# Transposed dense products of a two-layer decoder: high weights against high and low tokens in one 512-column matmul

## The chip, the cores and the metric

The kernel runs on one core of a Trainium2 chip. The time is device microseconds of one launch, the median of three runs. The engines are TensorE (PE in the profile, with its weight loads as PEld), VectorE (DVE), ScalarE (ACT), GpSimd (POOL) and SyncE (SP), whose queue issues the big loads.

## The reference

Two layers over 256 tokens of width 2048, in 32-bit floating point: a retention layer (A) and a dilated attention layer (B), each with a branch that attends to 256 fixed memory tokens. Nearly all the arithmetic is in the dense products with the weights.

```python
D_MODEL = 2048; SEQ = 256; DEPTH = 2; MEM_LEN = 256      # BATCH = 1
...
def rmsnorm(x, g):
    xf = x.astype(jnp.float32)
    y = xf * lax.rsqrt(jnp.mean(xf * xf, axis=-1, keepdims=True) + EPS) * g.astype(jnp.float32)
    return y.astype(x.dtype)
...
def retention_layer(x, g, w_in, w_mem_kv, w_out, mem_n):
    h = rmsnorm(x, g)
    q, k, v, gate_r, mq, gate_m = split_cols(h @ w_in, [RET_QK_W, RET_QK_W, RET_V_W, RET_V_W, MEM_W, MEM_W])
    ...
    o = retention(q, k, v.reshape(B, S, RET_HEADS, RET_DV))
    o = o * lax.rsqrt(jnp.mean(o * o, axis=-1, keepdims=True) + EPS)
    o_ret = o.reshape(B, S, RET_V_W).astype(x.dtype) * jax.nn.silu(gate_r)
    o_mem = memory_branch(mq, gate_m, mem_n, w_mem_kv)
    return x + jnp.concatenate([o_ret, o_mem], axis=-1) @ w_out
...
def dilated_layer(x, g, w_in, w_mem_kv, w_out, mem_n, kv):
    h = rmsnorm(x, g)
    parts = split_cols(h @ w_in, [DIL_W] * n_g + [DIL_W, MEM_W, MEM_W])
    ...                  # three (window, dilation) groups, merged by their softmax denominators
    o_mem = memory_branch(mq, gate_m, mem_n, w_mem_kv)
    return x + jnp.concatenate([o_dil, o_mem], axis=-1) @ w_out
...
def reference(x, mem, norm_a, w_in_a, w_out_a, norm_b, w_in_b, w_out_b, w_mem_kv, mem_norm_g, kv_norm_g, w_kv, final_norm_g):
    mem_n = rmsnorm(mem, mem_norm_g)
    x = retention_layer(x, norm_a[0], w_in_a[0], w_mem_kv[0], w_out_a[0], mem_n)
    kv = shared_kv(x, kv_norm_g, w_kv)          # rmsnorm(x) @ w_kv, cut into keys and values
    x = dilated_layer(x, norm_b[0], w_in_b[0], w_mem_kv[1], w_out_b[0], mem_n, kv)
    return rmsnorm(x, final_norm_g)
```

## The kernel before

**Three matmuls for one product.** A 32-bit product is made of parts that TensorE takes at its fast rate (type fp32r): each operand is split into a high part and the low rest (`split`, L73: ScalarE copies to the high part, VectorE subtracts). A product is then high x high + high x low + low x high, three matmuls into one accumulator.

**Two kinds of dense product.** `dense` (L242) makes 512 output columns of the tokens times a weight matrix, over a contraction of 2048 (16 blocks of 128) or 3072 (the two out-projections). With `transposed=True`, called a *column product* here, the weights are the stationary operand and the 256 tokens stream: for each block of 128 x 512 weights there are four column groups (`ct`) with three matmuls of 256 columns each (`mm3`, L77 to L80). There are 44 such products. Otherwise, a *row product*, the tokens are stationary and 512 weight columns stream (`row_part`, L248 to L252).

**Weights.** `weights` (L216) loads raw tiles of 128 x 1024 (two blocks, 512 KB) through SyncE's queue into a ring of five (`wraw`), and splits each 512-wide block into a ring of four pairs (`wspl`: `wh`, `wl`). Where a norm's gain is folded into the weights (layer B: `w_b`, `w_kv`), ScalarE scales with a per-partition gain (L237) and VectorE subtracts with the same gain (L238); elsewhere a plain `split` is used. Splits are marked with a priority of 100, so the tile framework's scheduler moves them ahead of work that is written before them.

**Order of the work.** The products follow one another on TensorE. All the rest (attention, statistics, transposes) is written as generators in `pending`; after each weight block `step()` takes one piece from the first of them, so that attention's matmuls lie between those of the next products. Accumulators `acc` are four PSUM banks, a product takes two. At the end of a product its result leaves PSUM through `cols_plain`, `cols_plain2`, `cols_scaled`, `gate_cols` or `rotary` for column products.

**Sequence.** Memory keys of layer A (two column products, whose tokens arrive meanwhile: `SplitCols`, L168, splits them at L184 and L185), memory values, the same for layer B, then layer A's products with memory attention and `retention`, the out-projection with transposes of the result (`turn_cols`, L530) and the norm of layer B (`norm_y`, L630), then for each of four head groups three query and three key column products, three value row products and a gate, with `dilated` attention (L469) of one group lying beside the first column products of the next. The second out-projection and the final norm end the kernel.

## Time and profile before

| | |
|---|---|
| median of 3 runs | 1940.17 us (1940.11 to 1940.19) |
| profiled execution, first to last instruction (span) | 1937.8 us |
| what lies around the span, against the median | 2.4 us |
| TensorE busy | 1925.1 us (99%) |
| VectorE busy | 1181.4 us (61%) |
| ScalarE busy | 1054.4 us (54%) |
| mean granted TensorE clock | 0.998 |
| read from memory | 345.80 MB, 180 GB/s over the span |

The profiled execution's own time is its span; the few microseconds around it are the launch, and are taken from the median of the runs. Busy is the share in which an instruction of the engine was running. Matmuls are pipelined, so their durations overlap, and a busy TensorE isn't a TensorE at its peak: the pitch from one start to the next tells its pace.

### The profile page before, as it was taken

To read this page: it belongs to the slowest core of one execution; us is meant where nothing else is said; L and a number is where in the kernel's file an instruction comes from. 1 tells how busy PE (TensorE), PEld (TensorE's weight loads), DVE (VectorE), ACT (ScalarE), POOL (GpSimd) and SP (SyncE) were. 2 spreads that over 40 slices of the span, in tenths; PEclk is the share of its full clock that TensorE was granted. 3 is DMA by queue.
4 is the path that set the end of the run, shared out by engine and by line. 5 is a ranking of instruction groups with operands and counts; after the bars stand their busy time and mean duration, and the time that the engine had idled before them with its cause. 6 is when DMAs were issued, how large, how long until landed. Compare 5 with 4: busy or idle time off the path is not lost.

```text
span 1937.8 us, 33224 instructions
## 1 busy us (share of the span) xinstructions
PE 1925.1 (99%) x12952; PEld 1785.4 (92%) x12952; DVE 1181.4 (61%) x1871; ACT 1054.4 (54%) x1731; POOL 12.2 (1%) x24
## 2 busy tenths in 40 slices
PE   9999999999999999999999999999999999999998
PEld 9898999889888889999989999899998999989886
DVE  6666557667666566665556655566555665556754
ACT  6556445555555455555555555555555555556544
POOL 0000000000000000000000000000000000000000
PEclk9999999999999999999999999999999999999999
DMA  7565544554555555445554355553555535555454
GB/s 267 184 228 187 184 159 159 203 181 167 200 186 199 202 185 175 164 163 177 185 195 175 134 183 184 196 175 131 185 178 194 183 134 181 182 195 175 150 200 144
DMA packets 98909, 350.06 MB, mean 181 GB/s; under 512 B 11088, under 2 KB 11648, under 8 KB 98752
## 3 DMA queue, kind: packets, MB, share of 16 engines
q1 hardware_dynamic: 98288, 347.12, 51.5%
q8 instruction: 101, 1.65, 0.3%
q0 software_dynamic: 320, 0.81, 0.1%
q14 instruction: 56, 0.46, 0.1%
q10 hardware_dynamic: 144, 0.01, 0.0%
HBM read 345.80 MB, written 2.10 MB: 180 GB/s over the span
## 4 chain that ended last, share of the span: by engine, by line
PE 98%; issue 1%; DVE 0%; DMA 0%; ACT 0%; POOL 0%; SPq 0%; ACTq 0%; POOLq 0%; DVEq 0%
PE acc L79 17%; PE acc L80 17%; PE acc L78 17%; PE acc L252 13%; PE acc L250 13%; PE acc L251 13%; PE att L79 1%; PE att L80 1%; PE att L78 1%; PE att L499 1%; PE att L477 1%; PE att L513 1%; DMA big<-in_memt_dram 0%; PE att L536 0%; PE att L451 0%
## 5 line engine op out<-in xcount | busy, mean ns | idle before, releaser
L78 PE MATMUL acc<-big,wh 128*128 128x256 f32 x2816 | 803.1, 285 | 1.7 <-ACT big L184 1.7
L80 PE MATMUL acc<-big,wl 128*128 128x256 f32 x2816 | 797.9, 283 | 0.0
L79 PE MATMUL acc<-big,wh 128*128 128x256 f32 x2816 | 797.6, 283 | 0.3 <-DVE big L185 0.3
L238 DVE SCALAR_TENSOR_TENSOR wl<-raw,gain,wh 128x512 fp32r<-128x512 f32 x704 | 528.4, 751 | 410.2 <-ACT wh L237 407.9
L237 ACT ACTIVATE wh<-raw,gain 128x512 fp32r<-128x512 f32 x704 | 509.0, 723 | 443.7 <-PE acc L79 311.3
L75 DVE TENSOR_TENSOR wl<-raw,wh 128x512 fp32r<-128x512 f32 x564 | 388.4, 691 | 275.1 <-ACT wh L74 273.3
L78 PEld LDWEIGHTS acc<-big,wh 128*128 128x128 f32 x2816 | 540.9, 192 | 2.2 <-ACT big L184 1.9
L79 PEld LDWEIGHTS acc<-big,wh 128*128 128x128 f32 x2816 | 541.2, 192 | 0.8 <-DVE big L185 0.5
L80 PEld LDWEIGHTS acc<-big,wl 128*128 128x128 f32 x2816 | 540.9, 192 | 0.0
L74 ACT CAST wh<-raw 128x512 fp32r<-128x512 f32 x564 | 349.8, 621 | 346.8 <-DVE wl L75 175.9
L250 PE MATMUL acc<-wh,big 128*128 128x512 f32 x1128 | 441.5, 391 | 0.0
L251 PE MATMUL acc<-wl,big 128*128 128x512 f32 x1128 | 439.3, 389 | 0.0
L252 PE MATMUL acc<-wh,big 128*128 128x512 f32 x1128 | 439.2, 389 | 0.0
L252 PEld LDWEIGHTS acc<-wh,big 128*128 128x128 f32 x1128 | 211.7, 188 | 44.3
L251 PEld LDWEIGHTS acc<-wl,big 128*128 128x128 f32 x1128 | 211.9, 188 | 42.4
L250 PEld LDWEIGHTS acc<-wh,big 128*128 128x128 f32 x1128 | 211.9, 188 | 42.4
L485 ACT ACTIVATE p<-sm,mn 128x512 f32<-128x512 f32 x32 | 23.1, 721 | 21.3 <-DVE mn L481 21.2
L75 DVE TENSOR_TENSOR big<-big 128x512 fp32r<-128x512 f32 (+1 forms) x34 | 28.4, 846 | 9.8 <-ACT big L74 9.7
L78 PE MATMUL att<-big 128*128 128x256 f32 x112 | 31.9, 285 | 0.0
L80 PE MATMUL att<-big 128*128 128x256 f32 x112 | 31.7, 283 | 0.0
L79 PE MATMUL att<-big 128*128 128x256 f32 x112 | 31.7, 283 | 0.0
L74 ACT CAST big<-big 128x512 fp32r<-128x512 f32 (+1 forms) x34 | 24.9, 745 | 11.7 <-DVE big L391 6.5
(150 smaller groups left out, 815.2 us busy)
## 6 DMA issues: line engine op xcount, KB each, us to landing
raw<-in_w_kv_dram SPq DMA_DIRECT2D x192, 512.0 KB, 3.6
raw<-in_w_b_dram SPq DMA_DIRECT2D x160, 512.0 KB, 3.6
raw<-in_w_a_dram SPq DMA_DIRECT2D x128, 512.0 KB, 3.6
raw<-in_w_mem_dram SPq DMA_DIRECT2D x60, 512.0 KB, 4.3
raw<-in_w_oa_dram SPq DMA_DIRECT2D x48, 512.0 KB, 3.7
raw<-in_w_ob_dram SPq DMA_DIRECT2D x48, 512.0 KB, 4.3
raw<-in_w_mem_dram SPq DMA_DIRECT2D x8, 256.0 KB, 7.7
big<-in_xt_dram SPq DMA_DIRECT2D x4, 512.0 KB, 6.5
```

The costliest lines, as they stand in the source:

```text
L74: act.copy(hi, src)
L75: dve.tensor_tensor(lo, src, hi.bitcast(F32), ALU.subtract)
L78: pe.matmul(o, lhsT=ah, rhs=bh, start=first, stop=False, skip_group_check=True)
L79: pe.matmul(o, lhsT=ah, rhs=bl, start=False, stop=False, skip_group_check=True)
L80: pe.matmul(o, lhsT=al, rhs=bh, start=False, stop=last, skip_group_check=True)
L237: act.activation(wh, src, AF.Copy, scale=gs)
L238: dve.scalar_tensor_tensor(wl, src, gs, wh.bitcast(F32), ALU.mult, ALU.subtract)
L250: pe.matmul(ps[t], lhsT=hi[:, a, ts], rhs=wh, start=first, stop=False)
L251: pe.matmul(ps[t], lhsT=hi[:, a, ts], rhs=wl, start=False, stop=False)
L252: pe.matmul(ps[t], lhsT=lo[:, a, ts], rhs=wh, start=False, stop=last)
L477: pe.matmul(ps[:, P + i * P:2 * P + i * P], lhsT=q[i][:, hd, ts], rhs=k[i][:, hd, ts], start=False, stop=(i == 2), skip_group_check=True)
L485: act.activation(p, sm, AF.Exp, bias=mn, scale=-1.0, accum_out=ls)
```

## The change

**Tokens side by side.** The token operand of a column product is stored as [128, 2, 2, 256]: for a block of the contraction the high and the low tokens stand next to each other (`cols_pair`, `xh`, `xl`, `xhl`).

**Two matmuls instead of three.** `dense_cols` multiplies a 128 x 128 piece of the high weights with the high and low tokens in one matmul of 512 columns, into a whole PSUM bank, and the low weights with the high tokens in one of 256 columns into the bank's first half. The result is the sum of the bank's two halves: `fold` copies the low half out (ScalarE) and adds the high half (VectorE), and what followed before (scaling, gate, rotary, split) follows on the folded tile.

**Halves of a product.** A column product is now made in two halves of 256 output columns, each over the whole contraction and in two banks; `acc` holds two such tiles. A weight tile for it is 1024 columns wide, four contraction blocks of 256 columns, contiguous in memory. The split pairs are 1024 wide, in a ring of three instead of four of 512, the raw ring has six tiles instead of five. A tile without gains is split by one 1024-wide pair of instructions; one with gains needs four pairs of 256 in a column product and two of 512 in a row product. `step()` comes after each second block of 256 columns.

**Start.** The first four raw tiles hold the first half of the first product; all four parts of the memory tokens are loaded between them. The first result is folded without the norm's factor and scaled later (`scale_half`).

```diff
-LOAD = 2
-RAW = 5
+RAW = 6
...
-    wspl = ctx.enter_context(tc.tile_pool(name="wspl", bufs=4))
+    wspl = ctx.enter_context(tc.tile_pool(name="wspl", bufs=3))
...
-    acc = ctx.enter_context(tc.tile_pool(name="acc", bufs=4, space=bass.MemoryType.PSUM))
+    acc = ctx.enter_context(tc.tile_pool(name="acc", bufs=2, space=bass.MemoryType.PSUM))
...
+    def cols_pair():
+        return [big.tile([P, 2, 2, S], F32R, name="big") for _ in range(2)]
+
+    def xh(part, a):
+        return part[a // 2][:, a % 2, 0, :]
+
+    def xl(part, a):
+        return part[a // 2][:, a % 2, 1, :]
+
+    def xhl(part, a):
+        return part[a // 2][:, a % 2].rearrange("p h s -> p (h s)")
...
-    def weights(w, c, j, g, keep=False):
-        res = []
-        for i in range(4):
-            if i % LOAD == 0:
-                if loaded:
-                    raw = loaded.popleft()
-                else:
-                    raw = wraw.tile([P, LOAD, 512], F32, name="raw")
-                    sp.dma_start(out=raw, in_=w[c, j, :, i:i + LOAD, :])
...
+    def split_weights(src, g, k0, n, wh, wl):
+        with tc.high_priority(AHEAD):
+            if g is None:
+                split(wh, wl, src)
+                return
+            w = src.shape[-1] // n
+            for i in range(n):
+                cs = slice(i * w, (i + 1) * w)
+                gs = gain[:, g, k0 + i:k0 + i + 1]
+                act.activation(wh[:, cs], src[:, cs], AF.Copy, scale=gs)
+                dve.scalar_tensor_tensor(wl[:, cs], src[:, cs], gs, wh[:, cs].bitcast(F32), ALU.mult, ALU.subtract)
+
+    def weights(src, g, k0, n, keep=False):
+        fresh = not loaded
+        if fresh:
+            raw = wraw.tile([P, 1024], F32, name="raw")
+            sp.dma_start(out=raw, in_=src)
+        else:
+            raw = loaded.popleft()
...
+            wh = wspl.tile([P, 1024], F32R, name="wh")
+            wl = wspl.tile([P, 1024], F32R, name="wl")
+        w = 1024 // n
+        if fresh:
+            split_weights(raw, g, k0, n, wh, wl)
+        else:
+            for i in range(n):
+                cs = slice(i * w, (i + 1) * w)
+                split_weights(raw[:, cs], g, k0 + i, 1, wh[:, cs], wl[:, cs])
+        return [(wh[:, i * w:(i + 1) * w], wl[:, i * w:(i + 1) * w]) for i in range(n)]
+
+    def dense_cols(xs, w, c, evict, g=None):
+        for i in range(2):
+            ps = acc.tile([P, 2, 2, S], F32, name="acc")
+            for j in range(4):
+                part = xs[j]
+                for a, (wh, wl) in enumerate(weights(w[c, i, j], g, 4 * j, 4)):
+                    first, last = j == 0 and a == 0, j == 3 and a == 3
+                    for ct in range(2):
+                        cs = slice(ct * P, (ct + 1) * P)
+                        pe.matmul(ps[:, ct].rearrange("p h s -> p (h s)"), lhsT=wh[:, cs], rhs=xhl(part, a),
+                                  start=first, stop=False, skip_group_check=True)
+                        pe.matmul(ps[:, ct, 0, :], lhsT=wl[:, cs], rhs=xh(part, a),
+                                  start=False, stop=last, skip_group_check=True)
+                    if a % 2:
+                        step()
+            evict(i, ps)
...
-                if transposed:
-                    for ct in range(4):
-                        o = ps[ct // 2][:, (ct % 2) * S:(ct % 2 + 1) * S]
-                        cs = slice(ct * P, (ct + 1) * P)
-                        mm3(o, wh[:, cs], wl[:, cs], hi[:, a, :], lo[:, a, :], first and ct % 2 == 0, last and ct % 2 == 1)
...
+    def fold(out, ps):
+        act.copy(two(out), ps[:, :, 1, :])
+        dve.tensor_tensor(two(out), ps[:, :, 0, :], two(out), ALU.add)
...
-    def cols_scaled(ps, b):
+    def cols_scaled(b, *job):
         o = big_tile()
-        for i in range(2):
-            dve.tensor_tensor(two(half(o, i)), two(ps[i]), twice(b), ALU.mult)
+
+        def evict(i, ps):
+            fold(half(o, i), ps)
+            if b is not None:
+                scale_half(o, i, b)
+
+        dense_cols(*job[:3], evict, *job[3:])
         return o
...
+    for j in range(4):
+        loaded.append(wraw.tile([P, 1024], F32, name="raw"))
+        if j == 0:
+            for i in range(4):
+                sp.dma_start(out=ms.raw[0][:, i, :], in_=memt[:, 0, i, :])
+                sp.dma_start(out=loaded[0][:, i * S:(i + 1) * S], in_=w_mk[0, 0, 0, 0, :, i * S:(i + 1) * S])
+        else:
+            ms.load(j)
+            sp.dma_start(out=loaded[j], in_=w_mk[0, 0, 0, j])
...
-    ps = dense(ms, w_mem[0], 0, transposed=True)
+    mk0 = cols_scaled(None, ms, w_mk[0], 0)
```

What the scheduler makes of it, at three places. Numbers stand for the position in the engine's queue; the lines of the change are its own (L85 and L86 are the plain split, L137 a square of the statistics, L195 and L196 the split of the tokens, L236 and L237 the split of weights with a gain, L314 and L315 the fold).

ScalarE at the start of the kernel, before (L74 is the cast of a weight block, L126 a square of the memory tokens, L184 the split of the memory tokens):

```order
4 L74 CAST wh<-raw 128x512
5 L126 ACTIVATE sm<-big 128x512
6 L74 CAST wh<-raw 128x512
7 L184 ACTIVATE big<-big,gain 128x256 x2
8 L74 CAST wh<-raw 128x512
9 L184 ACTIVATE big<-big,gain 128x256
```
The same place in the change:

```order
4 L85 CAST wh<-raw 128x256
5 L137 ACTIVATE sm<-big 128x512
6 L85 CAST wh<-raw 128x256 x2
7 L137 ACTIVATE sm<-big 128x512
8 L85 CAST wh<-raw 128x256
9 L137 ACTIVATE sm<-big 128x512 x2
10 L85 CAST wh<-raw 128x256 x4
11 L195 ACTIVATE big<-big,gain 128x256 x5
12 L85 CAST wh<-raw 128x256 x4
```
The first token split stood behind two casts and one square; now it stands behind eight casts of 256 and four squares, and the last of the 16 behind a cast of 1024.

VectorE where layer B begins, before (L621 adds the out-projection to the residual, one for each half of the tokens, L632 begins the norm):

```order
370 L238 SCALAR_TENSOR_TENSOR wl<-raw,gain,wh 128x512 x2
371 L621 TENSOR_TENSOR big<-big,acc 128x512
372 L238 SCALAR_TENSOR_TENSOR wl<-raw,gain,wh 128x512
373 L621 TENSOR_TENSOR big<-big,acc 128x512
374 L238 SCALAR_TENSOR_TENSOR wl<-raw,gain,wh 128x512 x2
375 L632 TENSOR_REDUCE ss<-part 128x2
376 L147 TENSOR_SCALAR r_y<-ss 128x2
377 L154 TENSOR_SCALAR p<-ident,r_y 128x128
```
The same place in the change (L681 is the add, L692 begins the norm):

```order
337 L237 SCALAR_TENSOR_TENSOR wl<-raw,gain,wh 128x256 x8
338 L681 TENSOR_TENSOR big<-big,acc 128x512
339 L237 SCALAR_TENSOR_TENSOR wl<-raw,gain,wh 128x256 x4
340 L681 TENSOR_TENSOR big<-big,acc 128x512
341 L237 SCALAR_TENSOR_TENSOR wl<-raw,gain,wh 128x256 x4
342 L692 TENSOR_REDUCE ss<-part 128x2
343 L158 TENSOR_SCALAR r_y<-ss 128x2
344 L165 TENSOR_SCALAR p<-ident,r_y 128x128
345 L86 TENSOR_TENSOR big<-att,big 128x2x256 x2
```
Between the two adds stood one split of 512, now there are four of 256, a whole tile; four more follow ahead of the norm.

VectorE in dilated attention, before (L481 adds the mask and finds the minimum, L487 and L488 divide by the sum after ScalarE's exponent, L75 splits the transposed weights of attention):

```order
479 L481 ISA sm,mn<-att,mask_t,nsd_y 128x512
480 L481 ISA mn 128x1
481 L487 RECIPROCAL rl_11659<-ls_11657 128x1
482 L488 TENSOR_SCALAR p<-p,rl_11659 128x512
483 L238 SCALAR_TENSOR_TENSOR wl<-raw,gain,wh 128x512
484 L75 TENSOR_TENSOR pl<-att,ph 128x2x128
485 L238 SCALAR_TENSOR_TENSOR wl<-raw,gain,wh 128x512
```
The same in the change (L537, L543 and L544, L86):

```order
487 L537 ISA sm,mn<-att,mask_t,nsd_y 128x512
488 L537 ISA mn 128x1
489 L86 TENSOR_TENSOR pl<-att,ph 128x2x128
490 L543 RECIPROCAL rl_9454<-ls_9452 128x1
491 L544 TENSOR_SCALAR p<-p,rl_9454 128x512
492 L237 SCALAR_TENSOR_TENSOR wl<-raw,gain,wh 128x256 x4
```
Two splits of 512 in a unit have become four of 256 in one place; between the mask and the division, where VectorE waits for ScalarE, stands a split of attention at most.

## Rows read from the trace of the kernel before

**Rows 1.** The page: busy time by engine; the chain by engine.
```profile
PE 1925.1 (99%) x12952; PEld 1785.4 (92%) x12952; DVE 1181.4 (61%) x1871; ACT 1054.4 (54%) x1731; POOL 12.2 (1%) x24
...
PE 98%; issue 1%; DVE 0%; DMA 0%; ACT 0%; POOL 0%; SPq 0%; ACTq 0%; POOLq 0%; DVEq 0%
```

**Rows 2.** Groups by line: names, shapes, count | busy us, mean ns | idle before.
```profile
L78 PE MATMUL acc<-big,wh 128*128 128x256 f32 x2816 | 803.1, 285 | 1.7 <-ACT big L184 1.7
...
L79 PEld LDWEIGHTS acc<-big,wh 128*128 128x128 f32 x2816 | 541.2, 192 | 0.8 <-DVE big L185 0.5
```

**Rows 3.** Order in time (start us, us, what), TensorE, a column product.
```profile
900.02 0.28 PE L80 MATMUL acc<-big,wl 128*128 128x256 f32 x1
...
906.02 0.28 PE L79 MATMUL acc<-big,wh 128*128 128x256 f32 x1
```

**Rows 4.** Order in time, TensorE, a row product.
```profile
989.69 0.39 PE L250 MATMUL acc<-wh,big 128*128 128x512 f32 x1
...
999.89 0.39 PE L250 MATMUL acc<-wh,big 128*128 128x512 f32 x1
```

**Rows 5.** Windows: us; busy by PE PEld DVE ACT POOL; clock, DMA, GB/s.
```profile
880.00:900.00 20.00, 20.00 (x169) 20.00 (x168) 10.52 (x14) 11.02 (x17) 0.00 (x0) 1.00 0.51 182
...
980.00:1000.00 20.00, 20.00 (x90) 16.57 (x89) 12.25 (x17) 11.77 (x17) 0.00 (x0) 1.00 0.56 198
```

**Rows 6.** Splits in order of time, ScalarE then VectorE: 256 wide, 512 wide.
```profile
17.55 1.70 ACT L184 ACTIVATE big<-big,gain 128x256 fp32r<-128x256 f32 x4
...
18.36 1.67 DVE L185 SCALAR_TENSOR_TENSOR big<-big,gain 128x256 fp32r<-128x256 f32 x4
...
727.78 1.41 DVE L238 SCALAR_TENSOR_TENSOR wl<-raw,gain,wh 128x512 fp32r<-128x512 f32 x2
```

**Rows 7.** Groups by line: 1024-wide splits, evictions from PSUM.
```profile
L74 ACT CAST big<-big 128x1024 fp32r<-128x1024 f32 x10 | 10.4, 1045 | 3.0 <-DVE big L297 3.0
...
L75 DVE TENSOR_TENSOR big<-big 128x1024 fp32r<-128x1024 f32 x10 | 12.1, 1223 | 2.9 <-ACT big L74 2.9
...
L285 ACT COPY big<-acc 128x512 f32<-128x512 f32 x16 | 9.2, 576 | 0.9
...
L297 DVE TENSOR_TENSOR big<-acc,nb 128x512 f32<-128x512 f32 x32 | 20.5, 683 | 0.0
```

**Rows 8.** The start: token split; group to 11.94; matmul; window; DMA to 12.
```profile
6.64 0.91 ACT L184 ACTIVATE big<-big,gain 128x256 fp32r<-128x256 f32 x2
...
L78 PE MATMUL acc<-big,wh 128*128 128x256 f32 x8 | 2.8, 372 | 1.7 <-ACT big L184 1.7
...
11.95 0.28 PE L79 MATMUL acc<-big,wh 128*128 128x256 f32 x1
...
9.00:12.00 3.00, 3.00 (x16) 3.00 (x16) 1.09 (x2) 1.16 (x4) 0.00 (x0) 0.51 1.03 400
...
DMA packets 1889, 3.17 MB, mean 264 GB/s; under 512 B 373, under 2 KB 933, under 8 KB 1889
...
q0 software_dynamic: 320, 0.81, 22.5%
```

**Rows 9.** The turn to layer B in order of time: TensorE, VectorE.
```profile
719.59 0.64 PE L536 MATMUL att<-ident,big 128*128 128x128 f32 x4
...
722.31 0.29 DVE L154 TENSOR_SCALAR p<-ident,r_y 128x128 f32<-128x128 f32 x1 [0.80 <-POOL r_y L148]
```

**Rows 10.** Dilated attention: windows; VectorE in order of time.
```profile
1052.00:1064.00 12.00, 12.00 (x103) 11.82 (x102) 10.42 (x24) 8.29 (x18) 0.00 (x0) 1.00 0.43 154
...
1064.00:1076.00 12.00, 12.00 (x104) 12.00 (x104) 7.99 (x19) 6.95 (x15) 0.00 (x0) 1.00 0.25 89
...
1061.03 0.74 DVE L481 CUSTOM_DVE_ANT_0 sm<-att,mask_t,nsd_y 128x512 f32<-128x512 f32 x1
...
1062.66 0.17 DVE L487 RECIPROCAL rl<-ls 128x1 f32<-128x1 f32 x1 [0.88 <-ACT p L485]
...
1072.28 0.74 DVE L481 CUSTOM_DVE_ANT_0 sm<-att,mask_t,nsd_y 128x512 f32<-128x512 f32 x1
```

More of the change, by code (lines that the diff above doesn't have):

```diff
@@ L242, in dense @@
-    def dense(xs, w, c, g=None, transposed=False, order=(0, 1, 2, 3), both=None, after=None):
-        ps = [acc.tile([P, 512], F32, name="acc") for _ in range(2)]
+    def split_weights(src, g, k0, n, wh, wl):
[9 more added lines that the diff above has]
+                dve.scalar_tensor_tensor(wl[:, cs], src[:, cs], gs, wh[:, cs].bitcast(F32), ALU.mult, ALU.subtract)
@@ L244, in dense @@
+    def dense(xs, w, c, g=None, order=(0, 1, 2, 3), both=None, after=None):
+        pt = acc.tile([P, 2, 512], F32, name="acc")
+        ps = [pt[:, t, :] for t in range(2)]
         n = 4 * len(order)
@@ L256, in dense @@
                 drain()
-            hi, lo = xs[j]
-            keep = both is not None and k >= both
-            for a, (wh, wl) in enumerate(weights(w, c, j, g, keep)):
-                first, last = k == 0, k == n - 1
-                k += 1
-                if transposed:
-                    for ct in range(4):
-                        o = ps[ct // 2][:, (ct % 2) * S:(ct % 2 + 1) * S]
-                        cs = slice(ct * P, (ct + 1) * P)
-                        mm3(o, wh[:, cs], wl[:, cs], hi[:, a, :], lo[:, a, :], first and ct % 2 == 0, last and ct % 2 == 1)
-                else:
-                    row_part(0, hi, lo, a, wh, wl, first, last)
+            part = xs[j]
+            for u in range(2):
+                keep = both is not None and k >= both
+                for a, (wh, wl) in enumerate(weights(w[c, j, u], g, 4 * j + 2 * u, 2, keep), 2 * u):
+                    first, last = k == 0, k == n - 1
+                    k += 1
+                    row_part(0, part, a, wh, wl, first, last)
                     if keep:
-                        late.append((1, hi, lo, a, wh, wl, first, last))
+                        late.append((1, part, a, wh, wl, first, last))
                     else:
-                        row_part(1, hi, lo, a, wh, wl, first, last)
-                step()
-                if len(order) > 4 and k % 2 == 0:
+                        row_part(1, part, a, wh, wl, first, last)
                     step()
+                    if len(order) > 4 and k % 2 == 0:
+                        step()
         if after is not None:
@@ L324, in gate_rows, with gate_cols, evict @@
         return o
-    def gate_cols(ps, bh):
+    def gate_cols(bh, *job):
         o = big_tile()
-        for i in range(2):
+        def evict(i, ps):
             hv = half(o, i)
-            dve.tensor_tensor(two(hv), two(ps[i]), twice(bh), ALU.mult)
+            fold(hv, ps)
+            dve.tensor_tensor(two(hv), two(hv), twice(bh), ALU.mult)
             th = tmp.tile([P, 512], F32, name="sm")
@@ L333, in gate_cols, with rotary, evict @@
             dve.scalar_tensor_tensor(hv, th, 1.0, hv, ALU.add, ALU.mult)
+        dense_cols(*job[:3], evict, *job[3:])
         return o
-    def rotary(ps, cosr, sinr):
+    def rotary(cosr, sinr, *job):
         h, l = big_pair()
-        for i in range(2):
-            s_ = two(ps[i])
+        def evict(i, ps):
+            z = tmp.tile([P, 512], F32, name="p12")
+            fold(z, ps)
+            s_ = two(z)
             a = tmp.tile([P, 2, S], F32, name="p")
@@ L528, in dilated, with turn_cols @@
                 yield
-    def turn_cols(xr, h, l):
+    def turn_cols(xr, part):
         for i in range(2):
@@ L536, in turn_cols @@
                     pe.transpose(ps[:, ct * S + t * P:ct * S + (t + 1) * P], xr[:, t, cs], ident)
-            split(half(h, i), half(l, i), ps)
+            split(part[i][:, :, 0, :], part[i][:, :, 1, :], two(ps))
             yield
@@ L558, in stats_m @@
         yield
-        mk_a.append(split_big(cols_scaled(ps, n_m.b)))
+        for i in range(2):
+            scale_half(mk0, i, n_m.b)
+            yield
+        mk_a.append(split_big(mk0))
         yield
```

132 lines of the change are left out of this document (63 added, 69 removed).

## The prediction

> **What bounds the kernel now.** I read the page first: TensorE is busy 99% of the span and is 98% of the chain that ended last [rows 1]. Nothing else matters unless it makes TensorE wait, so the next view is what TensorE spends its time on. In the groups by line the matmuls of the dense products carry nearly everything: 2816 of each of L78, L79 and L80 with 256 moving columns, the column products, of which [rows 2] shows the first line; the row products (L250 to L252) stream 512. The mean durations (285 ns) overlap and must not be added: 8448 x 0.285 us is longer than the span. What counts is the pitch from one start to the next, which only the order in time shows. In a column product 50 matmuls start within 6.00 us, 0.1200 us each [rows 3]; in a row product 45 start within 10.20 us, 0.2267 us each [rows 4]. Twice the columns cost 0.1067 us more, so each matmul has a part of 0.1200 - 0.1067 = 0.0133 us that doesn't depend on its columns. The clock is granted in full in both stretches (1.00, the 2.4 GHz level) [rows 5].
>
> **Column products, the term that pays.** For a 128x128 piece of a weight block before issues three 256-column matmuls, 0.3600 us. The change issues one of 512 (high weights against high and low tokens side by side) and one of 256, 0.2267 + 0.1200 = 0.3467 us. The streamed columns are the same 768; what goes is one matmul's fixed part. There are 2816 such pieces: 2816 x 0.0133 = 37.5 us. No row shows long and short matmuls in turn. Bounds: a gain of 2816 x 0.12 = 338 us if the 512 cost no more than a 256, which the row products exclude; a loss of 2816 x (0.4534 - 0.3600) = 263 us if a short matmul next to a long one took the long one's pitch, for which nothing in either stream speaks. Between them stands 0, the fixed part coming back, a rival below. I take the pitches as they are: a 256 already follows a matmul with a weight load of its own at 0.120, so the rows of the same sizes are the nearest.
> What a matmul costs beyond its columns is told otherwise by the Trainium skill, "TensorE: Matmul & The Clock Gate", section "Back-to-back issue gap": a warm stream needs N/2.4 ns plus about 2.5 ns. By that rule 2816 matmuls fewer are worth an estimated 7 us, not 37.5. The rows here disagree, 120.0 and 226.7 ns against 109.2 and 215.8, and the sum goes by the rows.
> Row products and attention keep their matmuls: 0 us.
>
> **Splitting the weights.** It has to stay hidden behind TensorE. A tile is now 1024 columns and TensorE takes 8 x 0.3467 = 2.77 us for it (before, two 512 blocks took 2.88). In layer B each column tile has four gains, so its split becomes four 256-wide pairs (L236, L237). Back to back, 256 wide costs ScalarE and VectorE 0.40 us each (1.70 and 1.67 for four), a 512-wide VectorE one 0.66 [rows 6]: 1.60 us in place of 1.33 for a tile, of 2.77. With each wait exposed it is 4 x 0.48 to 0.50 = 2.0 us. Where no gain is folded in, one 1024-wide split replaces two, 1.05 and 1.22 us [rows 7], so that side gets lighter. The ring is three tiles deep: when one comes free, two more (5.5 us) are ready, and 2.5 us fill it again. Cost 0. The weights' bytes don't change; one tile in 2.77 us asks for 4% more than the 182 GB/s of [rows 5]. 0 us.
>
> **Leaving PSUM.** Each half of a column product (88 in all: 44 products, two halves) now has a ScalarE copy of the low part and a VectorE add, about 0.58 and 0.68 us by the nearest evictions [rows 7]. Both wait for the last matmul of the half; behind them on their engines stand the next weight splits, and TensorE waits for those. The order puts the fold behind three tiles already split, and the accumulator has two buffers of one half each, so the fold has the 8 x 0.3467 x 4 = 11.1 us of the next half. Hidden: 0 us. Without that cover it would be 88 x 1.26 = 111 us.
>
> **The start, a loss.** Before, the first product went over all 512 output columns while the memory tokens arrived; now the first half needs all tokens within 11.1 us of matmuls. Worse, the order puts four squares and the casts of two weight tiles ahead of the first token split (L195) on ScalarE. These need 2.1 MB, with 0.81 MB of tables on their way too; 3.17 MB had landed at 12 us [rows 8], so 2.9 MB is there at about 11.3, and the four casts of the second tile (at most 0.40 each) put the first token split at 12.9, where before it ran at 6.64 [rows 8]. From there ScalarE has 16 token splits and 8 casts (24 x 0.40) and a 1024-wide cast (1.05) before the last token split is done: 23.5 us. VectorE's part and the last two pairs (0.40 + 0.69) end the half at 24.6. It holds 11.1 us of matmuls, so 13.5 us are lost, and up to 15.0 if TensorE starts on the lower clock level again, as it did before (0.51 from 9 to 12 us). Before, TensorE was in step from 11.95 us with about 21 matmuls (8 of L78 by then, so 7 of each line) and thus 2.5 us of work behind it: 9.4 lost. Loss 4.1 to 5.6; I take 4.6. Bounds 0 (the loads arrive sooner) to 8.
>
> **The turn to layer B.** There TensorE needs the last residual chunk transposed and the norm spread. Before, VectorE added both halves with one 512-wide split between them, and the transposes began at 719.59 without a wait [rows 9]. Now four 256-wide splits stand between, and the second add, which the norm's chain needs, waits behind them. Counted from the last row product's end: the third tile's split ends at 2.2 us (4 x 0.40 on ScalarE, then 0.48 of VectorE and the hand-over), the second add at 2.9. Its square on ScalarE stands behind the fourth tile's split, which waits for TensorE to finish the first tile (2.8): about 5.2. Reduction, power and scaling take about 1.4 us more (VectorE waits 0.80 for the power and scales in 0.29 [rows 9], with two small steps ahead of them), so its first matmul can run at 6.6 and its second, behind 1.3 us of transposed splits, at 8.0; TensorE comes to them after 16 and 18 pairs and seven transposes, at some 6.2 and 7.1. That's 0.4 and 0.9 us of waiting: 1.3, and I take 1.4, bounds 0 to 4.
>
> **Attention beside column products.** Here VectorE is fullest: 18.4 of 24 us in the first dilated stretch. Two units of attention, with five `step()` calls, took 11.25 us there (1061.03 to 1072.28), 2.25 for a step with its block of weights; 10.7 steps in 24 us [rows 10]. Each step adds 2 x 0.40 - 0.66 = 0.14 us of splits and, eight steps to a half, 0.68/8 = 0.08 of folds: 18.4 + 10.7 x 0.22 = 20.7 of the 23.5 us that TensorE then needs, 88%. It still fits, unless VectorE's own waits cannot be filled. It waits 0.88 us in a unit for ScalarE's exponent [rows 10], and the new order leaves that wait as it was. Were all 5.6 idle us needed, 26.3 of 23.5 would be over by 2.8 in 24 us; four groups of 20 steps, 45 us each, make 4 x 45/24 x 2.8 = 21 us. The other end is 0. TensorE waited for nothing there before, and up to two tiles stand ready, so I take 5 us, a quarter, for dilated, memory attention and retention together.
>
> **Sum.** The profiled execution's span is 1937.8 us; the median of the runs is 1940.17, so 2.4 us lie around it and are not touched, nor is the end after the last matmul. 1937.8 - 37.5 + 4.6 + 1.4 + 5.0 = 1911.3, with the 2.4 us **1913.7 us**.
>
> **Rivals.** *All is hidden.* Attention and the turn cost nothing and the start 3 us: 1940.2 - 37.5 + 3 = 1905.7. For it: TensorE waits nowhere in the column stretches of before. Against: VectorE at 88%.
> *VectorE becomes the bound beside attention.* The full 21 us, with 4.6 and 3 at the turn: 1940.2 - 37.5 + 28.6 = 1931.3. For it: the wait of 0.88 us in every unit. Against: that stretch held its pitch at 10.4 of 12 busy.
> *The weight load comes out behind the short matmul, and the kernel is slower.* In each pair the next high weights must load while only 256 columns stream. A load is recorded with 192 ns and the 256-column stream has no room in its load row (20.00 of 20.00), the 512 stream has (16.57) [rows 2, 5]. If the pair costs 0.0133 us more for it, nothing is saved and the rest stays: 1940.2 + 11.0 = 1951. It decides from a pair of 0.3561 us, where the gain is smaller than 11.0 us. Against it: such loads already pass behind 256 columns at 0.120.
> By the Trainium skill's rule above the kernel would end on the same side, at an estimated 1940.2 - 7 + 11 = 1944; since the two pitches speak against it, that case gets no more than a third of this rival's chance.
>
> **How the numbers follow.** Forecast 0.52, all hidden 0.18, VectorE late 0.24, weight load 0.06. This kernel's measurement tells 0.2%, 4 us, from no change. The first three are all faster; the last is slower except for a piece near zero: faster 0.94, same 0.02, slower 0.04. The forecast's own terms run from 1902.7 (all losses 0) to 1935.7 (8, 4 and 21); the range, 1902 to 1932, leaves out the slow rival and a little at the far end.
>
> **What would show it.** The order in time inside a column product should show starts 0.227 and 0.120 apart; a sum of 0.36 refutes the main term. The granted clock should stay 1.00 after the start. The first token split should stand near 13 us and the second half's matmuls begin near 24.6. ScalarE's and VectorE's busy sums should rise by some 100 us or more and TensorE show idle time released by the splits of L237 and by L543, L544 in the dilated stretches: none means "all hidden", over 15 us the second rival. The forecast is wrong if the pair's pitch differs from 0.347, or if a wait stands at the end of every half.

## The result and the profile after

The changed kernel takes **1923.66 us** (median of 4 runs, 1922.74 to 1924.03) against 1940.18 us of the kernel before (1940.11 to 1940.34). The ratio is 0.9913, 95% interval 0.9899 to 0.9927. The forecast was 1913.7 us with a range of 1902 to 1932: the time lies in the range, and some 60% of the forecast gain came. The profiled execution's span is 1921.7 us (before 1937.8).

The page first: busy time by engine, then the chain by engine, to be held against [rows 1].

```profile
PE 1898.5 (99%) x10136; PEld 1630.3 (85%) x10136; DVE 1241.4 (65%) x2195; ACT 1094.5 (57%) x2039; POOL 12.2 (1%) x24
...
PE 97%; DVE 1%; issue 1%; ACT 0%; DMA 0%; POOL 0%; SPq 0%; ACTq 0%; POOLq 0%; DVEq 0%
```

TensorE still bounds everything, with 2816 matmuls fewer. VectorE rose by 60 us and ScalarE by 40, as forecast about 100 together. The new lines that answer to [rows 2] (count | busy us, mean ns | idle before):

```profile
L269 PE MATMUL acc<-big,wh 128*128 128x512 f32 x2816 | 998.0, 398 | 10.7 <-DVE big L196 10.7
L271 PE MATMUL acc<-big,wl 128*128 128x256 f32 x2816 | 787.7, 280 | 0.0
...
L269 PEld LDWEIGHTS acc<-big,wh 128*128 128x128 f32 x2816 | 529.6, 188 | 133.6 <-DVE big L196 11.0
```

What TensorE waits for says at once that most feared terms are not there (engine, line waited for: us in total, times, longest):

```profile
PE acc L269 <- DVE big L196: 10.7, 1, 10.7
PE att L507 <- DVE p L500: 1.2, 1, 1.2
PE att L117 <- DVE mhalf L121: 1.1, 1, 1.1
PE acc L286 <- DVE big L741: 0.8, 1, 0.8
PE att L166 <- DVE p L165: 0.7, 3, 0.3
```

No wait on a weight split (L237) and none in the dilated attention. The first line is the start, L507 lies in retention, L117 is the warm-up ahead of the first product, L286 the last out-projection, L166 the norms' spreading.

The windows that answer to [rows 5] and [rows 10] (busy by PE, PEld, DVE, ACT, POOL; clock, DMA share, GB/s) show the dilated stretch with VectorE at 21.5 of 24 us, TensorE without a gap and the clock at 1.00:

```profile
880.00:900.00 20.00, 20.00 (x115) 17.32 (x114) 13.81 (x33) 13.19 (x31) 0.00 (x0) 1.00 0.61 195
...
1052.00:1064.00 12.00, 12.00 (x83) 10.88 (x82) 10.93 (x29) 9.06 (x24) 0.00 (x0) 1.00 0.49 151
1064.00:1076.00 12.00, 12.00 (x83) 11.02 (x82) 10.56 (x28) 8.65 (x23) 0.00 (x0) 1.00 0.37 112
```

So the gain that is missing is not in waits but in the pace of the matmuls. The order in time on TensorE, at the place of [rows 3]: two high matmuls, 16 pairs apart.

```profile
900.03 0.40 PE L269 MATMUL acc<-big,wh 128*128 128x512 f32 x1
...
905.68 0.40 PE L269 MATMUL acc<-big,wh 128*128 128x512 f32 x1
```

That is 5.65/16 = 0.353 us a pair. And the same loop of the same kernel later, also 16 pairs:

```profile
1150.41 0.39 PE L269 MATMUL acc<-big,wh 128*128 128x512 f32 x1
...
1155.96 0.39 PE L269 MATMUL acc<-big,wh 128*128 128x512 f32 x1
```

Here it is 5.55/16 = 0.347, the pitch of the forecast. Over whole stretches the means are 0.3533 and 0.3467. Tiles, operands and clock are the same in both, and each stretch keeps its pace to its end, over as many as 352 pairs. By the starts of all L269, pairs of the undisturbed stretches divide nearly evenly (some 1220 at the shorter pace, some 1230 at the longer; the rest stand next to attention steps or in the start). The mean is 0.3500.

Where the time went, by the start of TensorE's first matmul of each stage, after minus before (us). "By 0.3467" is what the stage would have gained at the forecast pitch, 0.853 for each column product.

| stage | change | by 0.3467 |
|---|---|---|
| up to the first matmul (7.20, now 16.44) | +9.24 | 0 |
| two column products of layer A's memory keys | -2.43 | -1.71 |
| layer B's memory keys, 2 | -0.86 | -1.71 |
| layer A, first 6 column products | -2.08 | -5.12 |
| next 2 | -1.49 | -1.71 |
| row products with retention, out-projection A | +1.48 | 0 |
| layer B, first 10 column products | -3.66 | -8.53 |
| 7 products each of the next three groups | -5.42, -5.69, -5.42 | -5.97 each |
| last column product | -0.43 | -0.85 |
| to the last matmul | +0.82 | 0 |
| small rest | -0.2 | 0 |
| **all** | **-16.1** | **-37.5** |

### The profile page after: what moved, and what is told of

It reads as the page before. It is cut to its first block, busy times and chain, and to the rows that moved or that the text cites. A ratio compares the mean times of both kernels' runs of the same rounds, so it can differ in the third digit from the quotient of the medians.

```text
span 1921.7 us, 27294 instructions
## 1 busy us (share of the span) xinstructions
PE 1898.5 (99%) x10136; PEld 1630.3 (85%) x10136; DVE 1241.4 (65%) x2195; ACT 1094.5 (57%) x2039; POOL 12.2 (1%) x24
## 4 chain that ended last, share of the span: by engine, by line
PE 97%; DVE 1%; issue 1%; ACT 0%; DMA 0%; POOL 0%; SPq 0%; ACTq 0%; POOLq 0%; DVEq 0%
PE acc L269 34%; PE acc L271 17%; PE acc L286 13%; PE acc L288 13%; PE acc L287 13%; PE att L91 1%; PE att L90 1%; PE att L89 1%; PE att L569 1%; PE att L533 1%; PE att L555 1%; DMA big<-in_memt_dram 0%; DVE wl L86 0%; PE att L507 0%; PE att L435 0%
## 5 line engine op out<-in xcount | busy, mean ns | idle before, releaser
L269 PE MATMUL acc<-big,wh 128*128 128x512 f32 x2816 | 998.0, 398 | 10.7 <-DVE big L196 10.7
L271 PE MATMUL acc<-big,wl 128*128 128x256 f32 x2816 | 787.7, 280 | 0.0
L237 DVE SCALAR_TENSOR_TENSOR wl<-raw,gain,wh 128x256 fp32r<-128x256 f32 (+1 forms) x1216 | 567.2, 524 | 304.4 <-ACT wh L236 303.9
L236 ACT ACTIVATE wh<-raw,gain 128x256 fp32r<-128x256 f32 (+1 forms) x1216 | 567.2, 533 | 342.2 <-PE acc L269 175.8
L269 PEld LDWEIGHTS acc<-big,wh 128*128 128x128 f32 x2816 | 529.6, 188 | 133.6 <-DVE big L196 11.0
L86 DVE TENSOR_TENSOR wl<-raw,wh 128x1024 fp32r<-128x1024 f32 (+1 forms) x294 | 346.3, 1180 | 302.5 <-ACT wh L85 302.2
L271 PEld LDWEIGHTS acc<-big,wl 128*128 128x128 f32 x2816 | 531.8, 189 | 0.3
L85 ACT CAST wh<-raw 128x1024 fp32r<-128x1024 f32 (+1 forms) x294 | 298.0, 1017 | 385.0 <-PE acc L288 231.2
L286 PE MATMUL acc<-wh,big 128*128 128x512 f32 x1128 | 441.5, 391 | 0.0
L286 PEld LDWEIGHTS acc<-wh,big 128*128 128x128 f32 x1128 | 211.9, 188 | 43.1
L315 DVE TENSOR_TENSOR big<-acc,big 128x512 f32<-128x512 f32 x64 | 44.1, 690 | 0.0
L314 ACT COPY big<-acc 128x512 f32<-128x512 f32 x64 | 36.3, 567 | 0.0
L91 PE MATMUL att<-big 128*128 128x256 f32 x112 | 31.7, 283 | 0.0
L86 DVE TENSOR_TENSOR big<-big 128x512 fp32r<-128x512 f32 (+1 forms) x34 | 27.9, 844 | 3.5 <-ACT big L85 3.5
L85 ACT CAST big<-big 128x512 fp32r<-128x512 f32 (+1 forms) x34 | 24.6, 743 | 2.2 <-DVE big L571 2.0
```

The lines of the kernel that those rows point to most:

```text
L85: act.copy(hi, src)
L86: dve.tensor_tensor(lo, src, hi.bitcast(F32), ALU.subtract)
L91: pe.matmul(o, lhsT=al, rhs=bh, start=False, stop=last, skip_group_check=True)
L236: act.activation(wh[:, cs], src[:, cs], AF.Copy, scale=gs)
L237: dve.scalar_tensor_tensor(wl[:, cs], src[:, cs], gs, wh[:, cs].bitcast(F32), ALU.mult, ALU.subtract)
L269: pe.matmul(ps[:, ct].rearrange("p h s -> p (h s)"), lhsT=wh[:, cs], rhs=xhl(part, a), start=first, stop=False, skip_group_check=True)
```

## The experiments

The kernel before ran beside each: 1939.85 us (first four), 1940.26 (next four), 1939.76 (last two).

### Three short matmuls in the new layout

```diff
-  pe.matmul(ps[:, ct] (512 columns), lhsT=wh[:, cs], rhs=xhl(part, a))
+  pe.matmul(ps[:, ct, 0, :], lhsT=wh[:, cs], rhs=xh(part, a))
+  pe.matmul(ps[:, ct, 1, :], lhsT=wh[:, cs], rhs=xl(part, a))
```

> The changed kernel with its two matmuls put back to three of 256 columns (high x high, high x low into the second half of the bank, low x high); layout, halves, folds and splits stay changed. Theory (the stages of the two traces): all else that the change does costs 8.5 us at the start and 2 to 3 in single waits, so 1940.2 + 11 = 1951 us, with 0.120 us from start to start. Rival (my forecast's terms): 4.6 at the start and 6.4 in waits of attention and the turn, also 1951 in sum, but then TensorE must show some 5 us of waits in the dilated stretches. Rival (the rest is free): 1940.

Measured: 1949.56 us (1949.09 to 1950.16), ratio 1.005 (1.0033 to 1.0067). The pitch is back at 0.120, and the column stages after the start stand within 0.6 us of the kernel before. So all that the change does besides the long matmul costs 9.7 us. In the profiled execution of this run 8.7 are lost up to the first row product, 1.5 around retention and 0.8 at the end, and the other stages give back some 0.9 in sum. The long matmul alone brought 1949.56 - 1923.66 = 25.9 us.

### Two long, then two short

```diff
   for ct in range(2):
       pe.matmul(ps[:, ct] (512), lhsT=wh[:, cs], rhs=xhl(part, a))
+  for ct in range(2):
       pe.matmul(ps[:, ct, 0, :] (256), lhsT=wl[:, cs], rhs=xh(part, a))
```

> Per contraction block two long matmuls (512), then two short ones (256), in place of long, short, long, short. Theory (locked step): only where long and short alternate one by one does a pair settle at 0.3533 us or at 0.3467, as the matmul before the stretch decides; in twos each pair takes 0.3467 everywhere, some 10 us less than the changed kernel: 1913.5. Rival (a fixed price of 6.7 ns for each return from short to long): half of it stays, 0.350 a pair, 1918.5. Rival (traffic of the other engines sets the pace of a stage): 0.3533 and 0.3467 stay where they are, 1923.7.

Measured: 1918.37 us (1917.63 to 1919.01), ratio 0.9889 (0.9874 to 0.9904): 5.3 us under the changed kernel with the same matmuls in another order. In time on TensorE (x2: two matmuls in a row), from one group of two pairs to the eighth after it:

```profile
899.78 0.63 PE L269 MATMUL acc<-big,wh 128*128 128x512 f32 x2
...
905.35 0.63 PE L269 MATMUL acc<-big,wh 128*128 128x512 f32 x2
```

5.57/16 = 0.348 a pair, where the changed kernel had 0.353; and the mean is 0.3483 in every column stretch. The two paces are gone. The one that is left is not the 0.3467 of the sum of both pitches, which long and short one by one do reach in half of their pairs; but it is the same everywhere. The time is the one that was expected from a fixed price for each return (1918.5), its pitch of 0.350 is not.

### Eight long, then eight short

```diff
-  for a, (wh, wl): two pairs of (512, 256)
+  for a, (wh, wl): two of 512
+  step()
+  for a, (wh, wl): two of 256
+  step()
...
-    if a % 2: step()
```

> All eight long matmuls of a weight tile first, then its eight short ones. Locked step: 0.3467 a pair everywhere, 1913.5. Price for each return: an eighth of it stays, 1914.8. Traffic: 1923.7. If a short matmul has room for its weight load only behind a long one, eight shorts in a row could be slower than 0.120 each, but the kernel before shows 0.120 in such a row.

Measured: 1922.42 us (1921.48 to 1923.05), ratio 0.991 (0.9895 to 0.9924). The attention steps move with it: one comes behind the eight long matmuls, one behind the eight short ones. The pitch is nearly uniform here too, but about 0.349, and each of the three dilated groups gained 4.7 to 4.9 us where the order in twos gained 5.4 to 5.6. Fewer changes of width bring nothing more, so the pace is not a fixed price for each change. None of the expected times came: 1913.5 and 1914.8 were too low, and 1923.7 was for paces that stay, which they do not.

### Two plain 32-bit transposes ahead of each column product

```diff
 def dense_cols(xs, w, c, evict, g=None):
+    kick = bank()
+    for n in range(2):
+        pe.transpose(kick[:, n * P:(n + 1) * P], ident, ident)
```

> Ahead of each of the 44 column products two plain 32-bit transposes of the identity that nothing reads. Locked step: the stretches that began behind a row product at 0.3533 (102 to 150 us, 197 to 248, the gates of layer B) go to 0.3467, and with them all up to the next attention matmul; the transposes cost some 0.3 us each, 13 in all, so 1927 or more, and the verdict is read from the pitch. Traffic or addresses: 0.3533 stays there, 1937.

Measured: 1936.46 us (1935.88 to 1937.14), ratio 0.9983 (0.9974 to 0.9993). The stretches changed sides, in both directions. In time on TensorE (L272 is the 512-wide matmul here), 16 pairs near 805, where the changed kernel runs at 0.353:

```profile
805.16 0.39 PE L272 MATMUL acc<-big,wh 128*128 128x512 f32 x1
...
810.70 0.39 PE L272 MATMUL acc<-big,wh 128*128 128x512 f32 x1
```

5.54/16 = 0.346. And 16 pairs near 1150, where the changed kernel runs at 0.347:

```profile
1150.58 0.40 PE L272 MATMUL acc<-big,wh 128*128 128x512 f32 x1
...
1156.23 0.40 PE L272 MATMUL acc<-big,wh 128*128 128x512 f32 x1
```

5.65/16 = 0.353. The work of the other engines and the traffic are nearly those of the changed kernel at both places (800 to 820 us: VectorE 14.9 of 20 us and 196 GB/s, in the changed kernel 15.2 and 198; 1145 to 1165 us: 14.4 in both, 185 and 188), so they don't set the pace; it is set as a stretch begins on TensorE. But every product here begins behind the same two transposes, and its stretch still takes one pace or the other (most the longer one, which is a part of the longer time). That a plain 32-bit matmul brings the shorter pace is refuted.

### The short matmul first

```diff
+  pe.matmul(ps[:, ct, 0, :] (256), lhsT=wl[:, cs], rhs=xh(part, a))
   pe.matmul(ps[:, ct] (512), lhsT=wh[:, cs], rhs=xhl(part, a))
-  pe.matmul(ps[:, ct, 0, :] (256), lhsT=wl[:, cs], rhs=xh(part, a))
```

> Edit: in each pair the short matmul (low weights) comes first, the long one after it; only the short one of a group's first block carries the start flag. The pair's pitch is 0.3467 in some stretches of the changed kernel and 0.3533 in others, though tiles and traffic are alike. Theory A (the first matmuls of a stretch set the pace that is then kept): the stretches change sides, those behind row products run at 0.3467 and those behind the 32-bit matmuls at 0.3533; since two thirds of the slow stretches are behind row products, 1916 to 1922 us. Theory B (the pace of a long matmul behind a short one depends on which kind of TensorE work was last, not on the phase): the same stretches stay slow, 1922 to 1925.

Measured: 1924.13 us (1923.8 to 1925.04), ratio 0.9918 (0.9901 to 0.9934). Theory A falls for nearly all stretches: those behind row products and behind the attention matmuls of L91 keep the longer pace, those behind the 32-bit matmuls of L569 the shorter one. One long stretch does change sides: the first, 93 pairs of the first two products from 20.3 us on, runs at 0.3532 here and at 0.3467 in the changed kernel. 16 pairs near 903 (L271 is the 512-wide one here) take 5.65 us, as in the changed kernel:

```profile
902.70 0.40 PE L271 MATMUL acc<-big,wh 128*128 128x512 f32 x1
...
908.35 0.40 PE L271 MATMUL acc<-big,wh 128*128 128x512 f32 x1
```

### The first product with both halves side by side

```diff
-    mk0 = cols_scaled(None, ms, w_mk[0], 0)
+    ps0 = [acc.tile([P, 2, 2, S], F32, name="acc") for _ in range(2)]
+    for j in range(4):                      # blocks of the contraction outermost
+        for i in range(2):                  # both halves
+            ...
+    for i in range(2): fold(half(mk0, i), ps0[i])
...
-    for j in range(4):  (raw tiles: first half, j = 0 to 3)
+    for n in range(4):  (raw tiles: both halves of j = 0, then of j = 1)
```

> Edit: only the very first product. Both its halves are worked side by side, block of the contraction by block, so that TensorE needs the memory tokens at half the pace, and the loads are ordered the same way. Theory (the changed kernel's first matmul comes 9 us later and then waits for tokens, since its half product wants all four token parts in 5.5 us of matmuls; that is 6 to 8 us of the loss): 1916 to 1918 us, that is 6 to 8 us below the changed kernel's 1923.7; rest of the trace unchanged. Rival (the start is bound by the loads and by the squares ahead of the first token split, whatever the order of the product): 1922 to 1924, the first row product starting as late as in the changed kernel.

Measured: 1919.90 us (1919.1 to 1920.05), ratio 0.9894 (0.988 to 0.9909): 3.8 us under the changed kernel, half of what was expected and more than the rival allows. Windows of the start (columns as above), of the changed kernel:

```profile
9.00:12.00 3.00, 0.00 (x0) 0.00 (x0) 1.51 (x4) 1.03 (x2) 0.00 (x0) 0.64 1.02 368
12.00:15.00 3.00, 0.00 (x0) 0.00 (x0) 2.05 (x6) 2.77 (x7) 0.00 (x0) 0.50 1.02 412
15.00:18.00 3.00, 1.56 (x5) 1.37 (x6) 3.00 (x9) 3.00 (x10) 0.00 (x0) 0.50 1.02 414
```

and of this one:

```profile
9.00:12.00 3.00, 0.00 (x0) 0.00 (x0) 1.19 (x4) 1.83 (x5) 0.00 (x0) 1.00 1.01 370
12.00:15.00 3.00, 2.55 (x8) 2.17 (x9) 3.00 (x9) 3.00 (x10) 0.00 (x0) 1.00 1.02 406
15.00:18.00 3.00, 3.00 (x13) 2.62 (x12) 3.00 (x9) 2.72 (x9) 0.00 (x0) 1.00 1.04 421
```

TensorE's first matmul comes at 12.45 in place of 16.44 (before the change: 7.20), because the splits of the first tokens no longer stand behind squares and casts of later loads (L195 begins at 11.11 in place of 14.61). From 12.45 us on TensorE has no gap in this product. The windows give its clock as 1.00, and its matmuls contradict that (L646 is the 512-wide one of this product; four pairs, then three):

```profile
13.89 0.63 PE L646 MATMUL acc<-big,wh 128*128 128x512 f32 x1
...
16.45 0.63 PE L646 MATMUL acc<-big,wh 128*128 128x512 f32 x1
...
18.28 0.40 PE L646 MATMUL acc<-big,wh 128*128 128x512 f32 x1
...
19.34 0.40 PE L646 MATMUL acc<-big,wh 128*128 128x512 f32 x1
```

That is 0.640 us a pair up to some 17.4 us, as in the changed kernel where the granted clock was 0.50, and 0.353 afterwards. The first clock record in this run's trace lies at 17.39 us and says 1.00; for the time before there is none, and the windows show 1.00 where no record says otherwise. So this start too goes at the pace of the lower level (1.2 GHz) for its first seven pairs. The first row product begins 3.4 us later than in the kernel before, not 6.8.

### Both: halves side by side at the start, and the order in twos

> Edit: the side-by-side first product of the run before together with two long, then two short matmuls for each weight block everywhere. Theory (the two losses have nothing to do with each other, so their gains add): changed kernel 1923.7, less 5.3 for the order in twos, less 6 to 8 for the start: 1910 to 1912.5 us. Rival (the start is bound by the loads): 1917 to 1918.5.

Measured: 1914.27 us (1914.05 to 1914.79), ratio 0.9866 (0.9852 to 0.9881), the two edits together; the mean pitch in every column stretch is 0.3483. The gains add: 5.3 + 3.8 = 9.1 from the single runs, 9.4 measured. The expected 1910 to 1912.5 was too low by what the start had been overrated. In its start the clock was recorded (windows as above):

```profile
9.00:12.00 3.00, 0.00 (x0) 0.00 (x0) 1.61 (x5) 1.99 (x6) 0.00 (x0) 0.64 1.02 411
12.00:15.00 3.00, 2.55 (x8) 2.17 (x9) 3.00 (x9) 3.00 (x10) 0.00 (x0) 0.50 1.02 415
15.00:18.00 3.00, 3.00 (x15) 2.63 (x15) 3.00 (x9) 3.00 (x10) 0.00 (x0) 0.73 1.03 415
```

The clock is at its lower level (0.50, 1.2 GHz) from 12 to 15 us, and the same 8 matmuls start there as in the run with the side-by-side halves alone, where the windows say 1.00. The first row product begins at nearly the same time in both (59.94 and 60.45 us). ScalarE and VectorE are full in both, but TensorE has no gap behind its first matmul, so whether they would hold it back at the full clock is not shown.

### Splits 512 wide where no gain is folded in

```diff
 if g is None:
-    split(wh, wl, src)                      # 1024 wide
+    for each half of 512: split(wh[:, cs], wl[:, cs], src[:, cs])
```

> Edit: weight tiles without gains are split by two pairs of instructions 512 wide instead of one pair 1024 wide, as before the change; nothing else. Theory (the stretch of layer A's row products with retention and the out-projection is 1.5 us longer than before because ScalarE and VectorE are held by one 1024-wide split while a short step of retention waits): the waits of TensorE on VectorE in that stretch go, 1.0 to 1.5 us less in that stretch, 1922 to 1923 in all. Rival (the wait comes from the ring of three split tiles or from the folds): no change of that stretch.

A single run: 1921.12 us. What settles it is the stage: the row products with retention and the out-projection of layer A, 1.48 us longer than before in the changed kernel, are 0.16 longer here. The changed kernel's chain at that place (start, us, what) shows why:

```profile
590.12 0.24 ACT sm L493
...
590.40 0.19 ACT sm L493
590.59 0.95 ACT wh L85
...
591.57 1.23 DVE wl L86
592.79 0.16 DVE cf L495 x2
592.96 1.35 POOL cf L496 x2
```

Retention's small steps on VectorE (L495) stand behind one whole weight split, 0.95 us on ScalarE and 1.23 on VectorE, and GpSimd (L496) behind them; TensorE then waits for L500. Halved splits let the small steps through: TensorE's wait for L500, 1.2 us in the changed kernel, is not among the waits of this run.

### The three edits together

> Edit: the kernel with the side-by-side first product and the order in twos (1914.27 us), and in it the 512-wide splits of weight tiles without gains. Theory (the 1024-wide splits cost 1.3 us in the stretch of layer A's row products with retention, and nothing anywhere else): 1912.5 to 1913.3 us, that stretch 0.2 us longer than in the kernel before instead of 1.5. Rival (the 2.5 us that the one look at narrow splits showed are mostly the start's chance): no change of that stretch, 1914.

Measured: 1913.32 us (1912.05 to 1914.01), ratio 0.9863 (0.9848 to 0.9878). The stage around retention is 0.14 us longer than before instead of 1.47. The two kernels were timed beside different runs of before and the intervals of their ratios overlap, so the stage, not the total, shows the 1.3 us. The lowest median of the study, 10.3 us under the changed kernel.

### Each fold done twice

```diff
 def fold(out, ps):
+    for _ in range(2):
         act.copy(two(out), ps[:, :, 1, :])
         dve.tensor_tensor(two(out), ps[:, :, 0, :], two(out), ALU.add)
```

> Edit: the changed kernel with each fold done twice (the copy out of the low half and the addition of the high half are issued a second time onto the same tile), which doubles what the change adds to ScalarE and VectorE at the end of each half product: 88 more pairs of instructions, some 0.4 and 0.55 us each. Theory (the folds lie beside TensorE's work and a half product's banks come free long before they are wanted again): 1923.7 to 1925 us. Rival (VectorE bounds beside attention and at the ends of products): 0.5 us for each of the 88 folds that stands on the path, up to 1965.

Measured: 1924.82 us (1923.95 to 1925.49), ratio 0.9923 (0.9907 to 0.994). 1.2 us for 88 more folds, at an edge of what the runs can tell: the page shows VectorE with 1296.4 us in place of 1241.4 and ScalarE with 1136.8 in place of 1094.5, nearly 100 us of work that TensorE doesn't see. Leaving PSUM is hidden, as the forecast had it.

## Why the prediction was right or wrong, point by point

**Column products: right mechanism, size off, the term that decided.** The forecast said 0.2267 + 0.1200 = 0.3467 a pair "as they are", everywhere, 37.5 us. Half the pairs have that, the other half 0.3533. At the mean of 0.3500, 2816 x 0.0100 = 28 us. The three-short experiment, with the rest of the change in place, gives 25.9. The other 2 us were not traced one by one; the four products that lie beside memory attention gained 0.1 to 0.2 us each, where undisturbed ones at the longer pace gained 0.43. The forecast called itself wrong if the pitch differed from 0.347, and for half of the pairs it did. The step that missed is taking the pitch of two pure streams for that of their mixture: no row of before showed long and short in turn, and the bounds that were written down (0 and a loss) were right to stand.

What sets the pace is only half settled. Shown: it is a matter of the order of matmuls on TensorE (the same matmuls in twos run at 0.3483 without exception), it is fixed where a stretch begins and kept, and it can be flipped in both directions by putting something in front; the other engines and the traffic don't decide it. Not shown: which feature of the beginning chooses. Whether long or short comes first does not, but for the first stretch, and the kind of the instruction just ahead doesn't suffice.

By the rule of the Trainium skill, "TensorE: Matmul & The Clock Gate", section "Back-to-back issue gap", 2816 matmuls fewer were worth an estimated 7 us. That section gives the rule for the isolated gap and says that in a stream of weight loads and matmuls both set the spacing; here every matmul has a load of its own, so the 7 us stretch the rule beyond what the section says. The runs disagree with it: 25.9 us, between that and the rows' 37.5.

**The start: right direction, too small.** 4.6 forecast, 8.5 measured (6.8 later at the first row product, where two products should have gained 1.7), which is over the forecast's own bound of 8. The chain of the start shows the piece that was missed (start, us, what):

```profile
4.50 7.50 DMA big<-in_memt_dram
...
12.11 0.64 ACT sm L137
...
13.76 0.44 DVE sqsum L144
...
15.23 0.75 DVE wl L86 x2
15.99 0.41 DVE big L196
16.39 0.04 issue
16.44 0.80 PE acc L269
```

The forecast let the first token split wait for the second raw tile's casts at 12.9; in fact the second part of the tokens landed at 12.00, its squares (L137) came after that, and the split stood behind them:

```profile
14.61 2.10 ACT L195 ACTIVATE big<-big,gain 128x256 fp32r<-128x256 f32 x5
...
16.44 0.80 PE L269 MATMUL acc<-big,wh 128*128 128x512 f32 x1 [10.71 <-DVE big L196]
...
20.27 0.40 PE L269 MATMUL acc<-big,wh 128*128 128x512 f32 x1
...
29.29 0.40 PE L269 MATMUL acc<-big,wh 128*128 128x512 f32 x1
```

The second half's matmuls began at 29.29 in place of the forecast 24.6 (last row). Of these 4.7 us, 1.7 are the first split's delay (14.61 for 12.9). Another part is the clock: TensorE was idle from 5.7 us on, the clock was granted at 0.50 from 12 to 18 us, and the first six pairs took 3.83 us (16.44 to 20.27), 1.75 more than at 0.3467. The forecast had written down up to 1.5 for this and taken 0.5. From 20.27 on the other 26 pairs run at 0.3467 without a wait, 9.0 us. The side-by-side start paid the lower level too, as told above.

**The turn to layer B.** 1.4 forecast. The waits of L166, three in all, sum to 0.7; only the last, 0.33, is at the turn. With the three short matmuls the whole group of ten products with the turn in it is 0.6 us longer than before. So at most some 0.7.

**Attention beside column products.** 5.0 forecast, nothing measured in the dilated stretches: no wait there, with VectorE at 21.5 of 24 us (90%, forecast 88%). The wait for ScalarE's exponent, which the forecast took to stay as it was, is about half of what it had been in the stretch from 1052 to 1076 us (waits of VectorE, the kernel before and the changed one: us in total, times, longest):

```profile
DVE rl L487 <- ACT p L485: 2.7, 3, 0.9
```
```profile
DVE rl L543 <- ACT p L541: 1.4, 3, 0.5
```

The rival that VectorE becomes the bound fell with it. But a term stood elsewhere that the forecast had at nothing: 1024-wide splits were "lighter", and were so in sum, but each holds an engine for 1.0 to 1.2 us, and retention's chain of small steps paid 1.3 of it, where a step and not the sum counts.

**The end.** 0.8 us, not forecast. The last out-projection's held-back matmuls wait for VectorE's read of the first 512 columns (start, us, engine, line; idle before):

```profile
1903.90 0.69 DVE L741 TENSOR_TENSOR big<-big,acc 128x512 f32<-128x512 f32 x1 [10.60 <-PE acc L288]
...
1904.65 0.50 PE L286 MATMUL acc<-big 128*128 128x512 f32 x1 [0.78 <-DVE big L741]
```

Both token halves of a row product now share one tile of two banks, and before they had a tile each. That this sharing makes the wait was argued from the code; no run took it apart.

**The sum again.** 37.5 - 9.3 for the pace of half the pairs = 28.2 gained; 8.5 + 1.5 + 0.8 + 0.7 = 11.5 lost: 16.7 by these terms, 16.1 by the spans. Two groups of errors of nearly the same size and opposite sign, 5.7 us at attention and the turn that didn't come and 6.2 at the start, retention and the end that did, left the pace as nearly the whole difference to the forecast. That they cancel is luck.

**The rivals.** *All is hidden* had the sign on its side that was written down for it, no wait of TensorE for L237, L543 or L544 in the dilated stretches. Its time, 1905.7 us, was missed by 18, because the start cost 8.5 and not 3, waits stood at other places, and half the pairs took the longer pace. The slow one (the weight load comes out behind the short matmul) had the right place, the short matmul beside a long one, and said from which pair it would decide, 0.3561; even the longer pace stays under that. The loads show nothing of it: L269's are recorded with 188 ns, in the stretch from 880 to 900 they are busy 17.32 of 20 us.

## What to carry to other kernels

When a change mixes instructions of two sizes, the pitch of the pure streams is a bound and not the value: price the mixture with its own uncertainty, and read the pace in several stretches of the result before trusting one. The order within a block of matmuls is worth a trial of its own, here 5.3 us for moving one loop line. A wide instruction that is cheaper in sum can still cost where a chain of small steps on the same engine has to pass it, and a product cut in halves over its output wants all its input in half the time, which at the start of a kernel is when that input is still on its way.

## What was not expected of the hardware

- Alternating matmuls of 512 and 256 columns (fp32r, clock 1.00) run at one of two paces, 0.3467 or 0.3533 us a pair, chosen as a stretch begins and kept for up to 352 pairs. In twos they run at 0.3483, in eights at about 0.349.
- A granted clock of 1.00 in the windows can be a missing record. In the side-by-side run they say 1.00 from 9 to 18 us while TensorE's pairs start 0.640 us apart, as at a granted 0.50 in the changed kernel; the first clock record lies at 17.39 us, and the pairs change to 0.353 there. The run in twos shows the same (first record at 20.85 us, two pairs in 1.28 us until then). At a start the pitch of the matmuls has to confirm the column.
